# One block of a hybrid encoder: the mLSTM's matrix E scaled on VectorE alone, its transposes issued behind the next scores, the values' constant factor moved, the memory's steps in halves, and one step more in the gates' preparation

## The chip, the core and the metric

The kernel runs on one core of a Trainium2 chip, as one launch, in fp32. The metric is device time of one execution, in microseconds (us); the figure given for a kernel is the median over its runs. A profiled execution also gives a trace: every instruction of the engines TensorE (PE for matmuls, PEld for its weight loads), VectorE (DVE), ScalarE (ACT), GpSimd (POOL) and the DMA queues, with start, duration and what ended the idle time before it.

## The reference, cut to what matters

One layer over 512 tokens of width 1024, with three token mixers beside each other (a bidirectional mLSTM, a neighbourhood attention, a cross-attention into 256 memory tokens), a gated merge, and a convolutional feed-forward network. The change touches the mLSTM, 4 heads of width 128, forwards and backwards:

```python
q = q * (Dh ** -0.5)
inter_log = a + m_prev
m_j = max(inter_log, max(D))                    # D: causal log weights
P = exp(D - m_j) * (q @ k.T)
inter_w = exp(inter_log - m_j)
num = P @ v + inter_w * (C_prev @ q)
den = sum(P) + inter_w * (n_prev . q)
h = num / max(abs(den), exp(-m_j))
...
h = h_fw + h_bw
h = h * rsqrt(mean(h * h) + EPS) * norm_g
return sigmoid(o_pre) * h
```

The states C and n are carried from chunk to chunk: `C_new = decay * C + (wt * v)^T k`, `n_new = decay * n + wt^T k`.

## The kernel before

**The stream of matmuls.** Tokens lie along the free axis (512 columns), channels on the 128 partitions. Each projection is a sum over 8 slices of the width; each slice is three matmuls of 128x512 (`mm3`, L213 to L215), since weight and input are each held as a high and a low part. The low times low product is left out. The weights come in blocks by DMA; ACT makes the high part of a block (`wh`, L195), DVE the low part (`wl`, L196), one block ahead of the matmuls that use it. So TensorE has one long stream, and ACT and DVE supply it.

**The mLSTM between the projections.** The gates' preparation and the four heads are a generator, `ml_prep` and `ml_all`, that gives up control at every `yield`. The function `step(n)` adds n to a quota and runs one piece of the generator for each whole unit in it. The projections call it: `xaq` adds 1.25 behind each of its four tiles (`RB`), `o`, `naq` and `nak` add 1.25 a tile in quarters (behind slices 1, 3 and 5, and at the end), `memk` and `memv` add 0.7 a tile (`RM`), and the merge gates of the first branch add 1 a tile. What a piece issues stands behind the projection's matmuls issued so far, and ahead of those that follow; a scheduler then lays down an order for each engine, in which an instruction may come somewhat earlier or later than its place in the program. On each engine the order is then fixed. Some small work is put into a list, `late`, and issued by `flush()` at slices 1, 3 and 5 of a projection.

**The pieces.** The preparation has four: the log forget gates; the running sums and maxima, which are written to memory by two DMAs (`rd`); an empty one; then `pm`, which transposes the sums back (L616, read by ACT L620 and L621, where `em` holds the exponential of the negative maxima), together with the first head's `keys`. `keys` loads the two rows `R` of that head by DMA, spread over the partitions (queue of SP), transposes k (L676) and splits it. `spread`, run from `late`, spreads the chunk ends by a matmul (L629), copies them (L632) and makes the weights `wt`, the decays `dec` and the factors `num` from them (L634 to L650). Then each head has five pieces: `states`, and `weights_J` for the chunks J of 128 tokens, 0 to 3.

- `states` weighs the values (L694, L697, L698), makes the four chunk products (L716 and the `mm3` of 258 columns), and from them the running states C (ACT L728, DVE L730). For the first head it also adds the causal mask to `R` (L670).
- `weights_J` issues the scores (`kq`, L750) and the product with the state (L756, or an `mm3` of 258 columns). DVE multiplies W, which ACT made by exponentials (L740), by the scores and sums each row (L764), then takes the larger of the sum's absolute value and `em` (L767, L768), the reciprocal (L769) and the factors r (L770). ACT scales one direction of W into E (L771), DVE adds the other (L772). The part from the state goes to H (ACT L776, DVE L778).
- `turn_J` transposes E on TensorE (L786), and ACT copies the result back (L787). `values_J` multiplies it by the values `va` (L792), adds (L793) and sums squares (L795).
- Behind a head come the norm (DVE L799, the power on POOL L801, ACT L806) and `emit_y` (four transposes L814, L816, and the split for the output projection L219, L220).

A constant of the reference, 128^-0.5 / 4 in this kernel's scaling (`C_ML`), is a factor of the values `va`, of the row sums in L764, and, inverted, of the table `num`, which has a second half for E.

Of the kernel before, what the change touches and what calls it, by code (L numbers as in the profile page):

```python
# [17 lines left out]
P = 128  # L18
# [10 lines left out]
WARM = 14  # L29
RM, RB = 0.7, 1.25  # L30
RATE = 1.0
# [79 lines left out]
def hybrid_block(ctx, tc, xg, xT, memT, wflat, vecs, gbias, nabias, outa, outb, outc):  # L111
# [338 lines left out]
    SY.dma_start(gbf, gbias.partition_broadcast(P))  # L450
    rcc = cp.tile([P, NT], F32, name="rcc")
    V.tensor_scalar(rcc, rc, C_ML, None, op0=ALU.mult)

# [47 lines left out]
    va = va_u.rearrange("p (t h c) -> p t h c", t=4, h=4)  # L501
    G.memset(va[:, :, :, 128:129], C_ML)
    nav_d = dp.tile([S, 1024], F32R, name="nav_d")
    for c in range(3):
        n, nk = TMC[c], TMK[c]
        pss = [(mmps if c % 2 else atps)() for _ in range(NT)]
        for h in range(KT // nk):
            ws = weights(("tm", c, h))
            for t in range(NT):
                tsl = slice(t * P, (t + 1) * P)  # L510
                for k in range(nk):
                    kk = nk * h + k
                    ps = pss[t][:, :n]
                    mm3(ps, XH[kk][:, tsl], XL[kk][:, tsl], ws[k][0], ws[k][1], kk == 0, kk == KT - 1)
        for t in range(NT):
            ps = pss[t]
            if c == 0:
                V.scalar_tensor_tensor(Gt[:, t, :], ps[:, :16], rc[:, t:t + 1], gb, op0=ALU.mult, op1=ALU.add)
            if c < 2:
                o = 16 if c == 0 else 0  # L520
                A.activation(va[:, t, 2 * c:2 * c + 2, 0:128],
                             ps[:, o:o + 256].rearrange("p (h c) -> p h c", h=2), AF.Copy, scale=rcc[:, t:t + 1])
# [26 lines left out]
    def ml_prep():  # L549
# [48 lines left out]
        with tc.issue_after(st["pool"]):  # L598
            G.memset(cu[:36], 0.0)
        num = cp.tile([P, 2, 2, 4, 4], F32, name="num")  # L600
        with tc.issue_after(st["pool"]):
            G.memset(num, 1.0 / C_ML)
        V.tensor_tensor_scan(cu[0:4, :], on[0:4, :], lr[0:4, :], 0.0, op0=ALU.mult, op1=ALU.add)
# [7 lines left out]
        yield  # L611
        yield
        pm = atps()
        pmv = pm[:, :400].rearrange("p (t c) -> p t c", t=NT)
        for t in range(NT):
            PE.transpose(pmv[:, t, :], mr[:100, t * P:(t + 1) * P], ident[:100, :100])  # L616
        em = cp.tile([P, NT, 36], F32, name="em")
        cp.tile([P, NT, 30], F32, name="gap2")

        A.activation(lfc, pmv, AF.Copy)  # L620
        A.activation(em, pmv[:, :, 0:36], AF.Exp, scale=-1.0)  # L621

        def spread():
# [18 lines left out]
            br = cp.tile([P, 2, 4, 4], F32, name="br")  # L642
            sc = [num[:, 1, 0, 1:4], num[:, 1, 1, 0:3]]
            for d in range(2):
# [11 lines left out]
    def ml_all():  # L656
# [48 lines left out]
        def states(h, k, w, C, q, R, ee):  # L705
# [6 lines left out]
            at = lambda J, d: pc[J // 2][:, po[J] + 129 * d:po[J] + 129 * d + 129]  # L712
            for J in range(NT):
                if J in (0, 3):
                    e = J // 3
                    PE.matmul(at(J, e), ke[:, e * P:(e + 1) * P], ew[e], start=True, stop=True)  # L716
# [26 lines left out]
        def weights_J(H, ss, h, J, k, w, C, q, R, ee):  # L743
# [5 lines left out]
            kq = ps[:, 384:512]  # L749
            PE.matmul(kq, qT[:, hs], kT[:, hs], start=True, stop=True)  # L750
            if len(ds) == 2:
                qs = slice((J - 1) * P, J * P)
# [5 lines left out]
            E = ee[:, J % 2 * 256:J % 2 * 256 + 256].rearrange("p (x c) -> p x c", x=2)  # L758
            y = tiny(8)
            init, den, r = y[:, 0:2], y[:, 2:4], y[:, 4:8].rearrange("p (x d) -> p x d", x=2)  # L760
            dd = slice(ds[0], ds[-1] + 1)
            V.tensor_tensor(init[:, dd], pi[:, dd, 128], num[:, 1, dd, J, h], op=ALU.mult)
            for d in range(2):
                V.tensor_tensor_reduce(W[:, d, :], W[:, d, :], kq, C_ML, init[:, d:d + 1] if d in ds else 0.0,  # L764
                                       ALU.mult, ALU.add, accum_out=den[:, d:d + 1])
# [3 lines left out]
            V.reciprocal(den, den)  # L769
            V.tensor_tensor(r, num[:, :, :, J, h], den.unsqueeze(1).to_broadcast([P, 2, 2]), op=ALU.mult)  # L770
            A.activation(E[:, 0, :], W[:, 0, :], AF.Copy, scale=r[:, 0, 0:1])  # L771
            V.scalar_tensor_tensor(E[:, 0, :], W[:, 1, :], r[:, 0, 1:2], E[:, 0, :], op0=ALU.mult, op1=ALU.add)  # L772
            src = None
            for d in ds:
                if src is None:
                    A.activation(H[:, js], pi[:, d, 0:128], AF.Copy, scale=r[:, 1, d:d + 1])  # L776
                else:
                    V.scalar_tensor_tensor(H[:, js], pi[:, d, 0:128], r[:, 1, d:d + 1], src, op0=ALU.mult, op1=ALU.add)  # L778
                src = H[:, js]
# [51 lines left out]
        for h in range(4):  # L831
# [261 lines left out]

    def paced(key):
        return proj(key, XH, XL, at={k: lambda: step(RB / 4) for k in (1, 3, 5)})

# [23 lines left out]
    for f in range(4):  # L1120
        ps = proj(("memk", f), MH, ML, M)
        V.tensor_tensor(mk[:, f * M:(f + 1) * M], ps[:, :M], mrb, op=ALU.mult)
        step(RM)
    pss = [mmps() for _ in range(2)]
    for i in range(4):
        ws = weights(("memv", i))
        for t in range(2):
            tsl = slice(t * P, (t + 1) * P)
            for k in range(2):
                kk = 2 * i + k  # L1130
                mm3(pss[t], MH[kk][:, tsl], ML[kk][:, tsl], ws[k][0], ws[k][1], kk == 0, kk == KT - 1)
        step(RM)
    for t in range(2):
# [3 lines left out]
    for f in range(4):  # L1137
        ps = paced(("naq", f))
        V.tensor_tensor(nq[:, f * S:(f + 1) * S].rearrange("p (b r c) -> p b r c", r=ROWS, b=4), rv(ps), rv(rb),
                        op=ALU.mult)  # L1140
        step(RB / 4)
    for f in range(4):
        ps = paced(("nak", f))
        V.scalar_tensor_tensor(nk[:, f * S:(f + 1) * S], ps, 0.125, rb, op0=ALU.mult, op1=ALU.mult)
        step(RB / 4)

# [378 lines left out]
```

## Time and profile before

| | |
|---|---|
| runs | 878.5, 881.27, 878.76 us |
| median | 878.76 us |
| profiled execution, its own time | 880.92 us |
| its span in the trace | 879.1 us |
| mean granted TensorE clock in it | 0.997 of full speed |

The span is the time from the first to the last instruction in the trace; 1.8 us of the profiled execution lie outside it. A row of a timeline gives the start, the duration, the engine, the line, what is written from what, the shape, and in brackets the idle time before the instruction with what ended it. Matmuls overlap: the time from one start to the next is what one costs, not its duration. Among rows of waits, the numbers are the total, the count and the longest. A row of windows has the stretch and its length, then busy time and count of PE, PEld, DVE, ACT and POOL, the granted clock of TensorE, the share of the DMA engines and their GB/s. The mLSTM lies between 100 and 245 us of the span.

### The profile page before, as it was taken

How to read it: one execution, taken by the hardware profiler on the slowest of the kernel's cores; microseconds unless marked ns; L12 is line 12 of the kernel's file. 1: busy time of each engine (PE TensorE's matmuls, PEld its weight loads, DVE VectorE, ACT ScalarE, POOL GpSimd, SP SyncE). 2: the span in 40 equal slices, each digit the busy share in tenths (PEclk: the TensorE clock that was granted, in tenths of full speed). 3: DMA queues.
4: the chain of work that ended last, by engine and by line, in shares of the span. 5: the costliest groups of instructions: out<-in, count | busy, mean ns of one | idle time of the engine just before them, and what ended most of it. 6: DMA issues, size and time to landing. Idle time of an engine off the chain costs nothing.

```text
span 879.1 us, 12264 instructions
## 1 busy us (share of the span) xinstructions
PE 869.4 (99%) x4287; PEld 734.7 (84%) x4287; DVE 598.3 (68%) x1316; ACT 476.4 (54%) x1005; POOL 125.1 (14%) x202
## 2 busy tenths in 40 slices
PE   9999999999999999999999999999999999999997
PEld 7898878888888888888888888888888888888887
DVE  7794788886667758898667649667633466666534
ACT  7563467775446658888634455444422344444532
POOL 0101100000071551700000001211100011111010
PEclk9999999999999999999999999999999999999999
DMA  8324633532252444533323432332233323222412
GB/s 280 99 78 156 198 116 84 163 121 85 85 144 79 113 129 141 159 112 109 120 89 108 142 103 86 102 114 96 66 101 97 120 97 96 96 96 91 127 47 97
DMA packets 39423, 99.82 MB, mean 114 GB/s; under 512 B 5689, under 2 KB 13881, under 8 KB 39361
## 3 DMA queue, kind: packets, MB, share of 16 engines
q1 hardware_dynamic: 31568, 92.32, 32.6%
q0 software_dynamic: 7360, 6.32, 3.4%
q8 instruction: 34, 0.56, 0.3%
q10 hardware_dynamic: 432, 0.39, 0.1%
q14 instruction: 29, 0.23, 0.1%
HBM read 94.80 MB, written 4.21 MB: 113 GB/s over the span
## 4 chain that ended last, share of the span: by engine, by line
PE 92%; DVE 3%; ACT 2%; DMA 2%; issue 1%; POOL 0%; SPq 0%; POOLq 0%; DVEq 0%
PE mm L215 27%; PE mm L213 27%; PE mm L214 27%; PE at L214 2%; PE at L213 2%; PE at L215 2%; DMA R<-rd 1%; PE at L953 1%; PE at L934 1%; PE at L915 0%; DVE wl L196 0%; PE at L916 0%; DMA wr<-wflat 0%; ACT wh L195 0%; PE at L1041 0%
## 5 line engine op out<-in xcount | busy, mean ns | idle before, releaser
L213 PE MATMUL mm<-u,wh 128*128 128x512 f32 (+1 forms) x1072 | 415.4, 388 | 0.1
L215 PE MATMUL mm<-u,wl 128*128 128x512 f32 (+1 forms) x1072 | 412.2, 385 | 0.0
L214 PE MATMUL mm<-u,wh 128*128 128x512 f32 (+1 forms) x1072 | 412.2, 385 | 0.0
L195 ACT ACTIVATE wh<-wr 128x512 fp32r<-128x512 f32 (+2 forms) x298 | 184.7, 623 | 213.3 <-PE mm L214 169.1
L196 DVE TENSOR_TENSOR wl<-wr,wh 128x512 fp32r<-128x512 f32 (+3 forms) x300 | 204.3, 682 | 91.5 <-ACT wh L195 87.9
L215 PEld LDWEIGHTS mm<-u,wl 128*128 128x128 f32 x1072 | 201.6, 188 | 40.1 <-DVE wl L196 0.2
L214 PEld LDWEIGHTS mm<-u,wh 128*128 128x128 f32 x1072 | 202.0, 188 | 38.5
L213 PEld LDWEIGHTS mm<-u,wh 128*128 128x128 f32 x1072 | 201.7, 188 | 38.6 <-ACT wh L195 0.5
L1389 POOL TENSOR_TENSOR s<-s,rb 128x512 f32<-128x512 f32 x22 | 38.1, 1734 | 402.5 <-DVE s L1388 238.9
L542 POOL DMA_DIRECT2D u<-nav_d x128 | 62.3, 506 | 67.4 <-PE at L953 22.4
L219 ACT ACTIVATE u<-s 128x512 fp32r<-128x512 f32 x26 | 16.5, 634 | 59.8 <-DVE s L1392 56.2
L1392 DVE TENSOR_TENSOR s<-mm,s 128x512 f32<-128x512 f32 x22 | 15.2, 691 | 23.9 <-POOL s L1389 23.9
L462 ACT ACTIVATE s<-pad,vec 128x512 f32<-128x512 f32 x30 | 24.5, 816 | 9.8 <-DVE pad L460 9.8
L220 DVE SCALAR_TENSOR_TENSOR u<-s,u 128x512 fp32r<-128x512 f32 x26 | 19.1, 734 | 14.1 <-ACT u L219 14.0
L463 DVE SCALAR_TENSOR_TENSOR s<-pad,vec,s 128x512 f32<-128x512 f32 x30 | 22.5, 751 | 5.6 <-ACT s L462 5.5
L1388 DVE SCALAR_TENSOR_TENSOR s<-s,s 128x512 f32<-128x512 f32 x22 | 15.2, 691 | 13.4 <-ACT s L1387 13.3
L464 DVE SCALAR_TENSOR_TENSOR s<-pad,vec,s 128x512 f32<-128x512 f32 x30 | 22.5, 751 | 0.8
L1387 ACT ACTIVATE s<-s 128x512 f32<-128x512 f32 x22 | 14.0, 634 | 14.9 <-DVE s L1386 14.9
L460 DVE TENSOR_TENSOR pad<-mm,rb 128x512 f32<-128x512 f32 x22 | 15.1, 690 | 6.3 <-PE mm L215 6.2
L1167 DVE TENSOR_TENSOR s<-mm,rb_x 128x512 f32<-128x512 f32 x16 | 11.0, 689 | 12.1 <-PE mm L215 12.1
L1399 DVE TENSOR_TENSOR u<-mm,u 128x512 f32<-128x512 f32 x13 | 9.0, 692 | 14.6 <-PE mm L215 14.6
L213 PE MATMUL mm<-wh,u 128*128 128x512 f32 x48 | 18.8, 392 | 0.0
(338 smaller groups left out, 1077.6 us busy)
## 6 DMA issues: line engine op xcount, KB each, us to landing
wr<-wflat SPq DMA_DIRECT2D x141, 512.0 KB, 3.4
nab<-nabias SPq DMA_DIRECT2D x16, 256.0 KB, 2.9
u<-nav_d POOLq DMA_DIRECT2D x128, 32.0 KB, 2.8
s<-xT SPq DMA_DIRECT2D x15, 256.0 KB, 4.0
wr<-wflat SPq DMA_DIRECT2D x14, 192.0 KB, 2.4
nav_d<-nv POOLq DMA_DIRECT2D x8, 256.0 KB, 3.4
R<-rd SPq DMA_DIRECT2D x8, 256.0 KB, 5.0
wr<-wflat SPq DMA_DIRECT2D x2, 544.0 KB, 3.4
```

What stands on the lines that cost most here:

```text
L195: A.activation(h[:, u:v], src, AF.Copy)
L196: V.tensor_tensor(l[:, u:v], src, h[:, u:v].bitcast(F32), op=ALU.subtract)
L213: PE.matmul(ps, lh, rh, start=start, stop=False)
L214: PE.matmul(ps, lh, rl, start=False, stop=False)
L215: st["mm"] = PE.matmul(ps, ll, rh, start=False, stop=stop).ins
L219: A.activation(h, src, AF.Copy, scale=scale)
L220: V.scalar_tensor_tensor(l, src, scale, h.bitcast(F32), op0=ALU.mult, op1=ALU.subtract)
L462: A.activation(t1, pad[:, 0:512], AF.Identity, scale=vcol(w, i), bias=vcol(b, i))
L463: V.scalar_tensor_tensor(t1, pad[:, 1:513], vcol(w, n + i), t1, op0=ALU.mult, op1=ALU.add)
L464: V.scalar_tensor_tensor(t1, pad[:, 2:514], vcol(w, 2 * n + i), t1, op0=ALU.mult, op1=ALU.add)
L542: G.dma_start(vw[r * 32:(r + 1) * 32, i * 256:(i + 1) * 256], nav_v[hf, r, CW[b]:CW[b] + 32, hp * 256:(hp + 1) * 256])
L1389: G.tensor_tensor(c, c, rb2, op=ALU.mult)
```

## The change

1. The values lose their constant factor: `va` is scaled by the plain norm `rc`, its extra column is 1, and the operation on `rcc` goes. The row sums in L764 take a factor 1. In its place `em` is multiplied by 1/C_ML on DVE, once, in a new operation of 128x144.
2. `num` loses the half for E and its memset on POOL. E's first direction is scaled on DVE by the reciprocal itself (new L770), the second is added behind it (new L771), and r for the state's part is made by a `tensor_tensor` between the two (new L772). ACT's L771 goes.
3. `turn_J` moves into `weights_J`, behind the next chunk's scores; it was ahead of `emit_y` and of `weights_J`.
4. The products in `states` come in the order of chunks 0, 3, 1, 2.
5. The preparation has one empty piece more. `memk` and `memv` add their 0.7 in two halves, `naq` and `nak` add 1.3 a tile (`RN`).
6. An unused filler tile in the small pool grows from 30 to 40 columns.

```diff
-RM, RB = 0.7, 1.25
+RM, RB, RN = 0.7, 1.25, 1.3
...
-    rcc = cp.tile([P, NT], F32, name="rcc")
-    V.tensor_scalar(rcc, rc, C_ML, None, op0=ALU.mult)
...
-    G.memset(va[:, :, :, 128:129], C_ML)
+    G.memset(va[:, :, :, 128:129], 1.0)
...
-        num = cp.tile([P, 2, 2, 4, 4], F32, name="num")
-        with tc.issue_after(st["pool"]):
-            G.memset(num, 1.0 / C_ML)
...
         yield
         yield
+        yield
         pm = atps()
...
+        V.tensor_scalar(em, em, 1.0 / C_ML, None, op0=ALU.mult)
...
-            for J in range(NT):
+            for J in (0, 3, 1, 2):
...
             PE.matmul(kq, qT[:, hs], kT[:, hs], start=True, stop=True)
+            if open_J:
+                turn_J(*open_J[0])
...
-                V.tensor_tensor_reduce(W[:, d, :], W[:, d, :], kq, C_ML, init[:, d:d + 1] if d in ds else 0.0,
+                V.tensor_tensor_reduce(W[:, d, :], W[:, d, :], kq, 1.0, init[:, d:d + 1] if d in ds else 0.0,
...
-            V.tensor_tensor(r, num[:, :, :, J, h], den.unsqueeze(1).to_broadcast([P, 2, 2]), op=ALU.mult)
-            A.activation(E[:, 0, :], W[:, 0, :], AF.Copy, scale=r[:, 0, 0:1])
-            V.scalar_tensor_tensor(E[:, 0, :], W[:, 1, :], r[:, 0, 1:2], E[:, 0, :], op0=ALU.mult, op1=ALU.add)
+            V.tensor_scalar(E[:, 0, :], W[:, 0, :], den[:, 0:1], None, op0=ALU.mult)
+            V.scalar_tensor_tensor(E[:, 0, :], W[:, 1, :], den[:, 1:2], E[:, 0, :], op0=ALU.mult, op1=ALU.add)
+            V.tensor_tensor(r[:, dd], num[:, dd, J, h], den[:, dd], op=ALU.mult)
...
-                turn_J(*open_J[0])
                 if J == 2 and last:
                     emit_y(h - 1, last[0])
                 open_J.append(weights_J(*prev, h, J, *own))
...
-        ps = proj(("memk", f), MH, ML, M)
+        ps = proj(("memk", f), MH, ML, M, at={3: lambda: step(RM / 2)})
...
-        step(RM)
+        step(RM / 2)
...
-        step(RM)
+            step(RM / 2)
...
-    ps = paced(("naq", f))
+    ps = paced(("naq", f), RN)
```

The matmuls are as many as before (4107 rows of TensorE). DVE has 17 rows more, ACT 18 fewer. Three places in the order of the engines follow; in the names, the number behind a name tells one buffer from another.

The first is DVE around the preparation's end, where `wt` is made and the first head's values are weighed: `at` is what L629 (new L626) spread, `R` the rows with their mask, `u_1294` (new `u_1291`) the split k, `s` and `ee` the weighed values. Before:

```order
L639 TENSOR_TENSOR bi<-Gt,lfc 128x16 x2
L645 TENSOR_TENSOR br<-lfc 128x16 x2
L670 TENSOR_TENSOR R_1284<-R_1284,msk_132 128x512
L685 TENSOR_TENSOR u_1294<-mm_1289,u_1294 128x256
L632 COPY mt<-at_1301 128x64
L670 TENSOR_TENSOR R_1286<-R_1286,msk_127 128x512
```

A few small rows make `wt` and `dec`, and then:

```order
L196 TENSOR_TENSOR wl_1373<-wr_1183,wh_1372 128x512
L670 TENSOR_TENSOR R_1357<-R_1357,msk_132 128x512
L694 TENSOR_SCALAR s_1295<-u_597,wt 128x129
L698 SCALAR_TENSOR_TENSOR u_1294<-u_597,wt,u_1294 128x129 x2
L694 TENSOR_SCALAR ee_1288<-u_597,wt 128x129
```

Now, the same stretch:

```order
L618 TENSOR_SCALAR em<-em 128x144
L683 TENSOR_TENSOR u_1291<-mm_1286,u_1291 128x256
L636 TENSOR_TENSOR bi<-Gt,lfc 128x16 x2
L643 TENSOR_TENSOR br<-lfc 128x16 x2
L668 TENSOR_TENSOR R_1281<-R_1281,msk_132 128x512
L629 COPY mt<-at_1315 128x64
L668 TENSOR_TENSOR R_1283<-R_1283,msk_127 128x512
```

```order
L196 TENSOR_TENSOR wl_1413<-wr_1225,wh_1412 128x512
L692 TENSOR_SCALAR s_1292<-u_595,wt 128x129
L696 SCALAR_TENSOR_TENSOR u_1291<-u_595,wt,u_1291 128x129 x2
L692 TENSOR_SCALAR ee_1285<-u_595,wt 128x129
L696 SCALAR_TENSOR_TENSOR u_1291<-u_595,wt,u_1291 128x129 x2
L668 TENSOR_TENSOR R_1401<-R_1401,msk_132 128x512
```

The split of k stands ahead of the first mask, not between it and the copy; the mask of the second head stands behind the weighed values, not ahead. On TensorE, the chunk products that read them (L716, new L714) come behind 24 matmuls of the `o` projection, where they came behind 19.

The second is DVE at the first head's third chunk: from the reciprocal (L769) to E (L772, new L771) and H (L778). Before:

```order
L769 RECIPROCAL y_1543<-y_1543 128x2
L762 TENSOR_TENSOR y_1601<-at_1598,num 128x1
L670 TENSOR_TENSOR R_1685<-R_1685,msk_132 128x512
L770 TENSOR_TENSOR y_1543<-num,y_1543 128x4
L764 ISA E_1555,y_1601<-E_1555,at_1598,y_1601 128x128
L764 ISA y_1601 128x1
L764 ISA E_1555,y_1601<-E_1555,at_1598 128x128
L764 ISA y_1601 128x1
L1116 TENSOR_SCALAR u_1404<-s_1571 128x512
L772 SCALAR_TENSOR_TENSOR ee_1288<-E_1479,y_1543,ee_1288 128x128
L778 SCALAR_TENSOR_TENSOR H_1412<-at_1538,y_1543,H_1412 128x128
```

Now:

```order
L769 RECIPROCAL y_1574<-y_1574 128x2
L770 TENSOR_SCALAR ee_1285<-E_1526,y_1574 128x128
L772 TENSOR_TENSOR y_1574<-num,y_1574 128x2
L771 SCALAR_TENSOR_TENSOR ee_1285<-E_1526,y_1574,ee_1285 128x128
L1105 TENSOR_TENSOR s_1608<-mm_1556,rb_x 128x512
L778 SCALAR_TENSOR_TENSOR H_1439<-at_1567,y_1574,H_1439 128x128
```

E follows the reciprocal by three rows on one engine; the mask, the next chunk's sums and the output gate's last operation no longer stand between.

The third is TensorE at the end of the last head: L792 makes the last values, L814 are the transposes of `emit_y`, and the rows between are the merge gates' projection. Before, the values are followed by twelve matmuls on `wh_2631` and twelve on `wh_2672` (with `wl_2673`), of which the first and the last stand here:

```order
L792 MATMUL at_2604<-u_597,ee_2312 128x128
L213 MATMUL mm_2680<-u_149,wh_2631 128x512
...
L215 MATMUL mm_2680<-u_149,wl_2632 128x512
L213 MATMUL mm_2730<-u_147,wh_2672 128x512
...
L215 MATMUL mm_2730<-u_147,wl_2673 128x512
L814 MATMUL at_2743<-ident,H_2440 128x128 x4
```

Now by twelve in all:

```order
L792 MATMUL at_2624<-u_595,ee_2340 128x128
L213 MATMUL mm_2716<-u_149,wh_2668 128x512
...
L215 MATMUL mm_2716<-u_149,wl_2669 128x512
L814 MATMUL at_2755<-ident,H_2451 128x128 x4
L213 MATMUL mm_2783<-u_1945,wh_2708 128x512
```

The transposes stand twelve matmuls closer to the values that they need.

More of the change, by code (lines that the diff above doesn't have):

```diff
@@ L521, in hybrid_block @@
                 A.activation(va[:, t, 2 * c:2 * c + 2, 0:128],
-                             ps[:, o:o + 256].rearrange("p (h c) -> p h c", h=2), AF.Copy, scale=rcc[:, t:t + 1])
+                             ps[:, o:o + 256].rearrange("p (h c) -> p h c", h=2), AF.Copy, scale=rc[:, t:t + 1])
             if c > 0:
@@ L617, in ml_prep @@
         em = cp.tile([P, NT, 36], F32, name="em")
-        cp.tile([P, NT, 30], F32, name="gap2")
+        cp.tile([P, NT, 40], F32, name="gap2")
         A.activation(lfc, pmv, AF.Copy)
         A.activation(em, pmv[:, :, 0:36], AF.Exp, scale=-1.0)
+        V.tensor_scalar(em, em, 1.0 / C_ML, None, op0=ALU.mult)
         def spread():
@@ L642, in spread @@
             br = cp.tile([P, 2, 4, 4], F32, name="br")
-            sc = [num[:, 1, 0, 1:4], num[:, 1, 1, 0:3]]
+            num = cp.tile([P, 2, 4, 4], F32, name="num")
+            sc = [num[:, 0, 1:4], num[:, 1, 0:3]]
             for d in range(2):
@@ L758, in weights_J @@
             E = ee[:, J % 2 * 256:J % 2 * 256 + 256].rearrange("p (x c) -> p x c", x=2)
-            y = tiny(8)
-            init, den, r = y[:, 0:2], y[:, 2:4], y[:, 4:8].rearrange("p (x d) -> p x d", x=2)
+            y = tiny(6)
+            init, den, r = y[:, 0:2], y[:, 2:4], y[:, 4:6]
             dd = slice(ds[0], ds[-1] + 1)
-            V.tensor_tensor(init[:, dd], pi[:, dd, 128], num[:, 1, dd, J, h], op=ALU.mult)
+            V.tensor_tensor(init[:, dd], pi[:, dd, 128], num[:, dd, J, h], op=ALU.mult)
             for d in range(2):
-                V.tensor_tensor_reduce(W[:, d, :], W[:, d, :], kq, C_ML, init[:, d:d + 1] if d in ds else 0.0,
+                V.tensor_tensor_reduce(W[:, d, :], W[:, d, :], kq, 1.0, init[:, d:d + 1] if d in ds else 0.0,
                                        ALU.mult, ALU.add, accum_out=den[:, d:d + 1])
@@ L775, in weights_J @@
                 if src is None:
-                    A.activation(H[:, js], pi[:, d, 0:128], AF.Copy, scale=r[:, 1, d:d + 1])
+                    A.activation(H[:, js], pi[:, d, 0:128], AF.Copy, scale=r[:, d:d + 1])
                 else:
-                    V.scalar_tensor_tensor(H[:, js], pi[:, d, 0:128], r[:, 1, d:d + 1], src, op0=ALU.mult, op1=ALU.add)
+                    V.scalar_tensor_tensor(H[:, js], pi[:, d, 0:128], r[:, d:d + 1], src, op0=ALU.mult, op1=ALU.add)
                 src = H[:, js]
@@ L1092, in hybrid_block, with paced @@
     gens.append(ml_all())
-    def paced(key):
-        return proj(key, XH, XL, at={k: lambda: step(RB / 4) for k in (1, 3, 5)})
+    def paced(key, rate=RB):
+        return proj(key, XH, XL, at={k: lambda: step(rate / 4) for k in (1, 3, 5)})
     xq = unit()
@@ L1137, in hybrid_block @@
     for f in range(4):
-        ps = paced(("naq", f))
+        ps = paced(("naq", f), RN)
         V.tensor_tensor(nq[:, f * S:(f + 1) * S].rearrange("p (b r c) -> p b r c", r=ROWS, b=4), rv(ps), rv(rb),
                         op=ALU.mult)
-        step(RB / 4)
+        step(RN / 4)
     for f in range(4):
-        ps = paced(("nak", f))
+        ps = paced(("nak", f), RN)
         V.scalar_tensor_tensor(nk[:, f * S:(f + 1) * S], ps, 0.125, rb, op0=ALU.mult, op1=ALU.mult)
-        step(RB / 4)
+        step(RN / 4)
     mg = []
```

## The prediction

> **What bounds the kernel now.** I read the page first, then the waits of TensorE, then the windows of the mLSTM's stretch, and last the timelines around each gap.
>
> ```profile
> PE 869.4 (99%) x4287; PEld 734.7 (84%) x4287; DVE 598.3 (68%) x1316; ACT 476.4 (54%) x1005; POOL 125.1 (14%) x202
> PE at L716 <- DVE s L694: 1.9, 1, 1.9
> PE at L786 <- DVE H L778: 1.2, 2, 1.0
> PE at L786 <- ACT wh L195: 1.0, 1, 1.0
> ```
>
> TensorE is busy for 99% of the span and the matmuls are as many afterwards, so only the gaps in its stream are to be won. The three longest kinds are all in the mLSTM: one wait for the weighed values, three for a transpose of E. DVE and ACT matter only where a row of theirs ends such a wait. The largest gap:
>
> ```profile
> 120.95 0.39 PE L215 MATMUL mm<-u,wl 128*128 128x512 f32 x1
> 121.18 0.39 PE L213 MATMUL mm<-u,wh 128*128 128x512 f32 x1
> 123.50 0.71 PE L716 MATMUL at<-s 128*128 128x129 f32 x2 [1.93 <-DVE s L694]
> ...
> 124.44 0.63 PE L214 MATMUL mm<-u,wh 128*128 128x512 f32 x1
> 124.86 0.63 PE L215 MATMUL mm<-u,wl 128*128 128x512 f32 x1
> 120.00:130.00 10.00, 8.07 (x35) 6.69 (x35) 8.33 (x28) 6.64 (x22) 0.00 (x0) 0.83 0.27 89
> ```
>
> A full-speed 128x512 matmul costs 0.23 us from start to start (120.95 to 121.18). L716 was due at 121.41 and came at 123.50: 2.09 us lost. Behind it the same matmul costs 0.42. The window's clock of 0.83 says that 0.17 x 10 = 1.7 us of clock are missing, which is half speed for about 3.4 us. So this one gap took 3.8 us in the profiled execution. The others:
>
> ```profile
> 146.07 0.39 PE L215 MATMUL mm<-u,wl 128*128 128x512 f32 x1
> 147.43 0.33 PE L786 MATMUL at<-ident,ee 128*128 128x128 f32 x1 [0.97 <-DVE H L778]
> ...
> 160.62 0.28 PE L214 MATMUL mm<-u,wh 128*128 128x256 f32 x1
> 161.94 0.30 PE L786 MATMUL at<-ident,ee 128*128 128x128 f32 x1 [1.04 <-ACT wh L195]
> ...
> 192.33 0.38 PE L792 MATMUL at<-u,ee 128*128 128x128 f32 x2
> 192.97 0.33 PE L786 MATMUL at<-ident,ee 128*128 128x128 f32 x1 [0.26 <-DVE H L778]
> 140.00:150.00 10.00, 9.03 (x50) 7.46 (x49) 9.07 (x38) 7.13 (x23) 0.84 (x1) 1.00 0.46 107
> ```
>
> Taking off what the matmul ahead costs (0.23 for 512 columns, 0.12 for 256, 0.11 for each of two passes of 128), the losses are 1.13, 1.20 and 0.42 us. The clock stayed at 1.00 through 140 to 150: a gap of 1.1 did not lower it, the one of 2.1 did. Together 2.09 + 1.13 + 1.20 + 0.42 = 4.84 us, and 1.7 of clock.
>
> **The first gap: where the weighed values come from.**
>
> ```profile
> 119.60 0.69 DVE L670 TENSOR_TENSOR R<-R,msk 128x512 f32<-128x512 f32 x1 [1.63 <-DMA R<-rd]
> 120.21 0.42 DVE L685 TENSOR_TENSOR u<-mm,u 128x256 fp32r<-128x256 f32 x1
> 120.55 0.21 DVE L632 COPY mt<-at 128x64 f32<-128x64 f32 x1
> ...
> 122.47 0.69 DVE L670 TENSOR_TENSOR R<-R,msk 128x512 f32<-128x512 f32 x1
> 123.07 0.29 DVE L694 TENSOR_SCALAR s<-u,wt 128x129 f32<-128x129 f32 x1
> ...
> 123.79 0.29 DVE L694 TENSOR_SCALAR ee<-u,wt 128x129 f32<-128x129 f32 x1
> ```
>
> DVE takes its rows in order. It stood 1.63 us idle at the first mask, until the DMA of `R` had landed at 119.60, with the copy of `mt`, on which `wt` hangs, behind that mask. Both versions issue that load with `keys` at the end of `xaq`, so I let the mask start at 119.60 again. What the change takes off DVE's path to the weighed values is two rows: the split of k (120.21 to 120.55, 0.34 us) now comes ahead of the mask, in the idle time, and the second head's mask (122.47 to 123.07, 0.60) comes behind. The new `em` row falls into the same 1.63 us and costs nothing here; without that cover it would cost its own 0.2 to 0.4. So `s` starts at 123.07 - 0.94 = 122.13. TensorE started 0.43 behind that row before (123.50 against 123.07), so it could start at 122.56; with five matmuls more ahead of it, it is due at 121.41 + 5 x 0.23 = 122.55. The first chunk product waits no longer. The second stands right behind now (chunks 0, 3, 1, 2), and reads `ee`, made 0.72 after `s`: ready at about 123.28, due at 122.55 + 0.22 = 122.77. That leaves a wait of 0.5 us, half of the 1.1 that the clock survived, so I keep the clock at full speed.
>
> The wait moves on partly. The state C of chunk 0 ends at
>
> ```profile
> 130.32 0.34 DVE L730 SCALAR_TENSOR_TENSOR C<-C,dec,at 128x129 f32<-128x129 f32 x1
> 130.72 0.49 PE L756 MATMUL at<-C,u 128*128 128x129 f32 x2
> 126.15 0.63 PE L716 MATMUL at<-ee,s 128*128 128x129 f32 x2
> ```
>
> that is, 4.5 us behind the start of the last chunk product (126.15 to 130.66). In the new order L756 stands 18 matmuls and one score behind it, 18 x 0.23 + 0.2 = 4.3 us, and DVE has rows of the `o` projection in between, as before. I take 0.4 us for it: nothing below, 1.0 above, if the second head's mask (0.60) falls into that chain too.
>
> **The three transposes.** Each gap ends with a chain that the change shortens:
>
> ```profile
> 159.03 0.16 DVE L770 TENSOR_TENSOR y<-num,y 128x4 f32<-128x4 f32 x1
> 160.71 0.39 ACT L771 ACTIVATE ee<-E,y 128x128 f32<-128x128 f32 x1
> 161.45 0.35 DVE L772 SCALAR_TENSOR_TENSOR ee<-E,y,ee 128x128 f32<-128x128 f32 x1
> 158.99 1.29 ACT L806 ACTIVATE H<-H,y 128x128 f32<-128x128 f32 x4 [1.37 <-POOL y L801]
> ```
>
> At 160 us the factors were there at 159.2, but ACT was in the norm's four scalings (to 160.28) and a weight split; E's first direction came at 160.71, its second at 161.45. On DVE alone E follows L770's place by one `tensor_scalar`, a small row and 0.35: ready by about 159.9, ahead of the 160.74 at which TensorE wanted it. At 146 a mask and the next chunk's sums stood between on DVE; they stand behind now. At 192 the hand-over to ACT and back goes. I take all three as gone, 1.13 + 1.20 + 0.42 = 2.75 us, and 0.1 for a last transpose that the new order puts close to its E; against it stands 0.16 for a like wait at 135 us, below.
>
> ```profile
> 135.21 0.40 PE L214 MATMUL mm<-u,wh 128*128 128x512 f32 x1
> 135.60 0.30 PE L786 MATMUL at<-ident,ee 128*128 128x128 f32 x1
> ```
>
> **What DVE takes over.**
>
> ```profile
> L771 ACT ACTIVATE ee<-E,y 128x128 f32<-128x128 f32 x16 | 6.3, 395 | 4.4 <-DVE y L770 4.2
> L772 DVE SCALAR_TENSOR_TENSOR ee<-E,y,ee 128x128 f32<-128x128 f32 x16 | 5.6, 349 | 3.7 <-ACT ee L771 3.7
> L694 DVE TENSOR_SCALAR s<-u,wt 128x129 f32<-128x129 f32 x4 | 1.1, 285 | 0.0
> 170.00:180.00 10.00, 10.00 (x57) 8.47 (x56) 9.86 (x37) 9.78 (x28) 0.00 (x0) 1.00 0.62 174
> ```
>
> ACT loses 16 x 0.395 = 6.3 us. The new `tensor_scalar` of 128x128 is not in the trace; its nearest row is L694, the same operation with a column more: 0.285, so 16 x 0.285 = 4.6 us on DVE. The bounds are 0.2 (the time from L694's start to the next one's, 123.07 to 123.26) and 0.35 (a two-input row, L772): 3.2 to 5.6 us. It lies beside TensorE's stream, which hides it as long as DVE has room. It has least at 170 to 180, with 9.86 of 10 us busy; TensorE lost nothing there, since the weight splits are a block ahead. Two chunks in 10 us add 0.6 there. I count nothing for it, and a rival below counts it. The factor moved into `em` and the memset that goes cost and bring nothing: they are off every wait shown.
>
> **The end of the last head.**
>
> ```profile
> 236.45 0.38 PE L792 MATMUL at<-u,ee 128*128 128x128 f32 x2
> ...
> 242.17 0.60 PE L814 MATMUL at<-ident,H 128*128 128x128 f32 x4
> 238.05 1.01 POOL L801 TENSOR_TENSOR y<-y,nhalf 128x4 f32<-128x4 f32 x1 [0.64 <-DVE y L799]
> 239.09 1.29 ACT L806 ACTIVATE H<-H,y 128x128 f32<-128x128 f32 x4 [1.50 <-POOL y L801]
> ```
>
> The norm's chain takes 239.09 + 1.29 - 236.45 = 3.9 us from the values to the last scaled chunk. There were 24 matmuls in it, 5.6 us; there are 12, so that the transposes are due 0.14 + 12 x 0.23 = 2.9 us behind. They go chunk by chunk, 0.11 each as other passes of 128: the last would come 2.9 + 0.33 = 3.2 behind and is ready at 3.9. That is a new wait of 0.7 us (0.4 to 1.0, by whether one of ACT's weight splits of 0.6 falls in front).
>
> **The sum.** New losses: 0.5 + 0.4 + 0.1 + 0.7 = 1.7 us. The 1.8 us of that execution outside its span I let stand. Against its 880.92: gained 4.84 + 1.7 + 0.16 = 6.7, so 880.92 - 5.0 = 875.9. The median of the runs is 878.76, 2.16 lower. The run of 881.27 stands near the profiled one, the other two near 878.6; the nearest thing that differs by such an amount is the 1.7 us of clock. I take it that the two lower runs kept the full clock. Against the median the clock's term then goes: 878.76 - 5.0 + 1.7 = 875.5. The two sums agree within 0.4, and I forecast 875.5, with 874.3 to 877.0 as this case's own range from the bounds above.
>
> The Trainium skill's page "TensorE: Matmul & The Clock Gate", section "Part 1: The HAM clock gate", has the clock switch between full and half rate by a free-running activity window of about 3.4 us, so that the same program may or may not be throttled. The stretch at half speed shown above, about 3.4 us, agrees. By that rule the two lower runs need not have paid; if they all had, the sum would be that of the first rival.
>
> **Rivals.**
>
> *A, more.* The runs of the median paid for the clock too, and differ from the profiled execution by something else; or the small new waits at the states and the end do not come. With the first, 6.7 gained less 1.7 lost: 878.76 - 5.0 = 873.8; with the second, 5.0 gained without the clock's term and nothing lost: 873.8 as well. For it: the trace shows one execution only, and it did pay. Against it: the two groups of runs lie 2.5 apart.
>
> *B, the first gap stays.* The mask that waits for `R` sets the chain, and that load may land later than 119.60, since its DMA shares queues with others; by a microsecond later the wait for `s` is 1 us, C follows, and the clock falls with them in some runs. Then of the 5.0 only the transposes' gain less the end's wait is left, 2.75 + 0.16 - 0.8 = 2.1: 876.7 without the clock's loss, 878.4 with it. For it: DVE was idle at that DMA for 1.63 us. Against: nothing in the change moves the load.
>
> *C, slower: DVE becomes the bound from the moment its rows per chunk fill what the matmuls leave.* E's chain is now wholly on DVE, in order, behind weight splits of 0.69 and masks; in the heads 1 to 3 ACT used to take a part of it while DVE split weights. If ten of the twelve transposes there each come 0.6 late (one split ahead of them), 6.0 us are lost, with the end's 0.7, and 2.9 gained at the old transposes and 0.5 at the first gap: 878.76 + 6.0 + 0.7 - 3.4 = 882.1. It decides once DVE is over about 9.9 of 10 us in a window, as it was at 170 to 180. For it: that row. Against: the same row had no loss on TensorE, and DVE's windows ahead show 8.3 and 9.1.
>
> *D, nothing.* The gaps only trade places: 878.8.
>
> **Chances.** The forecast 0.50, A 0.14, B 0.18, C 0.14, D 0.04. A measurement of this kernel can tell about 0.3%, 2.6 us, from no change: faster means below 876.1. A lies there whole, the forecast for three quarters of its range, B hardly: 0.14 + 0.38 + 0.02 = 0.54. Slower means over 881.4, which C reaches in about two thirds of its cases (nine late transposes or more): 0.10. The rest, 0.36, is no change. The range goes from 873.2, below A, to 878.6, above B; C and part of D lie outside.
>
> **What would show it.** In the new profile the wait at the chunk products (new L714) is at most 0.6 us and the clock around 120 to 130 is 1.00; a clock below that means that B holds. No wait of 0.3 us or more stands at L786, and one of 0.4 to 1.0 at L814 near 242 us. The new L770 takes 0.2 to 0.35 us. DVE is busy for some 4 to 5 us more and ACT for some 6 less. The forecast is wrong if waits at L786 add up to over 1 us (C), if `R`'s mask starts later than 120.5 (B), or if a gap appears outside 100 to 245 us, where I expect none.

## The result, and the profile after

| | before | changed |
|---|---|---|
| median of 7 runs | 880.53 us | 876.32 us |
| lowest to highest | 878.5 to 881.27 | 875.56 to 876.8 |
| profiled execution | 880.92 | 876.34 |
| its span | 879.1 | 874.6 |

The ratio is 0.9957, with a 95% interval of 0.9944 to 0.9969: 0.43% faster, 2.7 to 4.9 us. The forecast was 875.5. The median of before has risen from the 878.76 of three runs to 880.53 of seven, because four of the seven lie near 881; the experiments say why. One later execution of the changed kernel took 2262.04 us at a granted clock of 1.000 and is left out of every median here.

TensorE's waits in the changed kernel (total, count, longest), with the windows that answer to those of before; the row that stands apart is the kernel before at 160 to 170:

```profile
PE at L714 <- DVE s L692: 0.4, 1, 0.4
PE at L714 <- DVE ee L692: 0.3, 1, 0.3
120.00:130.00 10.00, 9.18 (x46) 7.29 (x45) 9.54 (x31) 8.44 (x27) 0.00 (x0) 1.00 0.45 154
140.00:150.00 10.00, 10.00 (x69) 9.08 (x69) 9.20 (x42) 6.93 (x21) 0.00 (x0) 1.00 0.58 157
160.00:170.00 10.00, 10.00 (x54) 8.61 (x53) 8.77 (x30) 7.96 (x23) 0.00 (x0) 1.00 0.54 155
170.00:180.00 10.00, 9.98 (x56) 8.39 (x55) 9.47 (x35) 8.20 (x26) 0.00 (x0) 1.00 0.50 163
```

```profile
160.00:170.00 10.00, 8.96 (x61) 8.07 (x60) 7.59 (x25) 7.25 (x20) 0.00 (x0) 1.00 0.47 159
```

No wait at the transposes (L786) is long enough to be listed; 140 to 150 and 160 to 170 are without a gap, where TensorE was busy for 9.03 and 8.96 of 10 us before. The clock is 1.00 from 120 to 130, where it was 0.83. What is left of the first gap stands in TensorE's timeline, and where it comes from in DVE's:

```profile
122.43 0.39 PE L215 MATMUL mm<-u,wl 128*128 128x512 f32 x1
123.25 0.46 PE L714 MATMUL at<-s 128*128 128x129 f32 x2 [0.43 <-DVE s L692]
123.97 0.46 PE L714 MATMUL at<-ee,s 128*128 128x129 f32 x2 [0.26 <-DVE ee L692]
```

```profile
118.40 0.23 DVE L618 TENSOR_SCALAR em<-em 128x144 f32<-128x144 f32 x1
118.55 0.42 DVE L683 TENSOR_TENSOR u<-mm,u 128x256 fp32r<-128x256 f32 x1
...
120.29 0.69 DVE L668 TENSOR_TENSOR R<-R,msk 128x512 f32<-128x512 f32 x1 [0.98 <-DMA R<-rd]
120.90 0.22 DVE L629 COPY mt<-at 128x64 f32<-128x64 f32 x1
...
122.83 0.28 DVE L692 TENSOR_SCALAR s<-u,wt 128x129 f32<-128x129 f32 x1
...
123.55 0.28 DVE L692 TENSOR_SCALAR ee<-u,wt 128x129 f32<-128x129 f32 x1
```

L714 was due at 122.43 + 0.23 = 122.66 and came at 123.25, 0.6 late; the second started 0.72 behind it, 0.5 later than the first's two passes of 0.11 allow. That is 1.1 us in all. DVE waits for the DMA of `R` as before, but it landed at 120.29, not 119.60. The new `em` row and the split of k lie in front of that wait. The new waits behind:

```profile
129.10 0.38 PE L748 MATMUL at<-u,u 128*128 128x128 f32 x2
129.62 0.49 PE L756 MATMUL at<-C,u 128*128 128x129 f32 x2
...
239.41 0.39 PE L215 MATMUL mm<-u,wl 128*128 128x512 f32 x1
239.75 1.21 PE L814 MATMUL at<-ident,H 128*128 128x128 f32 x4
240.71 0.48 PE L213 MATMUL mm<-u,wh 128*128 128x512 f32 x1
```

L748's two passes of 0.11 end at 129.32, L756 comes at 129.62: 0.3 for the state C. The four transposes of `emit_y` take 0.96 us from their start to the next matmul and came 0.1 late; before they took 0.35 (242.17 to 242.52): 0.7 lost in all. The new operation, in the rows of groups:

```profile
L770 DVE TENSOR_SCALAR ee<-E,y 128x128 f32<-128x128 f32 x16 | 4.8, 302 | 0.3
L771 DVE SCALAR_TENSOR_TENSOR ee<-E,y,ee 128x128 f32<-128x128 f32 x16 | 5.6, 347 | 0.0
PE 868.0 (99%) x4287; PEld 733.6 (84%) x4287; DVE 601.6 (69%) x1332; ACT 471.0 (54%) x989; POOL 125.1 (14%) x201
```

It takes 0.302 us. DVE is busy for 3.3 us more, with 16 rows more on the page (1316 before), and ACT for 5.4 us less, with 16 fewer (1005 before).

### The profile page after: what moved, and what is told of

It is laid out like the page before. It is cut to its first block, busy times and chain, and to the rows that moved or that the text cites. A ratio compares the mean times of both kernels' runs of the same rounds, so it can differ in the third digit from the quotient of the medians.

```text
span 874.6 us, 12276 instructions
## 1 busy us (share of the span) xinstructions
PE 868.0 (99%) x4287; PEld 733.6 (84%) x4287; DVE 601.6 (69%) x1332; ACT 471.0 (54%) x989; POOL 125.1 (14%) x201
## 4 chain that ended last, share of the span: by engine, by line
PE 93%; DVE 3%; DMA 1%; ACT 1%; issue 1%; POOL 0%; SPq 0%; POOLq 0%; ACTq 0%
PE mm L213 27%; PE mm L215 27%; PE mm L214 27%; PE at L214 2%; PE at L213 2%; PE at L215 2%; PE at L952 1%; DVE wl L196 1%; PE at L933 1%; DMA R<-rd 1%; DMA wr<-wflat 0%; PE at L914 0%; PE at L915 0%; PE at L1040 0%; PE at L792 0%
```

## The experiments

For every run the same four sums are read from TensorE's timeline, as above: the time from one start to the next, less what that step takes without a wait (0.23 for 512 columns, 0.12 for 256, 0.11 for 128, and 0.35 for the four transposes of L814). All in us:

| run | chunk products | C | transposes L786 | end L814 | median |
|---|---|---|---|---|---|
| before | 2.1, and the clock | 0 | 3.3 | 0 | 880.53 |
| changed | 1.1 | 0.3 | 0.4 | 0.7 | 876.32 |
| e0 before again | 2.9, and the clock | 0 | 3.0 | 0 | 880.28 |
| e1 E on ACT again | 0.6 | 0.3 | 0.9 | 0.7 | 876.65 |
| e2 only E on DVE | 1.9 | 0 | 0.6 | 0 | 876.61 |
| e3 steps as before | 1.0 | 0.2 | 2.5 | 0 | 877.33 |
| e4 turn ahead | 0.9 | 0.3 | 0.5 | 0.7 | 876.19 |
| e5 order 0123 | 1.6 | 0.2 | 0.4 | 0.7 | 876.05 |
| e6 second load later | 0 | 0.5 | 0.4 | 0.7 | 875.7 |
| e7 load, and 1.375 | 0 | 0.5 | 1.9 | 0 | 876.07 |
| e8 changed again | 0.5 | 0.3 | 0.4 | 0.7 | 876.26 |
| e9 1.301 | 0.4 | 0.3 | 0.4 | 0 | 874.87 |
| e10 1.301 and load | 0.3 | 0.3 | 0.4 | 0 | 875.22 |
| e11 H on DVE, steps as before | 1.1 | 0 | 1.7 | 0 | 876.44 |

A row's sums are of one execution, its median is of 5 to 10. That execution can lie off the median: e3's took 878.43 us, 1.1 above it, and e5's 877.09, the longest of its five. e0 to e3 ran beside each other, e4 to e7, and e8 to e10; the kernel before had medians of 879.0, 878.79 and 879.3 there, and 878.95 beside e11. Across these groups half a microsecond decides nothing.

**e0, the clock.** The kernel before, unchanged.

> The kernel before, unchanged, to see the granted clock of each run beside its time. If the two groups of its runs (near 878.6 and near 880.9) differ by the half-speed stretch behind the first gap, runs near 878.6 show a mean clock of 0.999 to 1.000 and runs near 880.9 one of 0.997 to 0.998. If something else parts them, the clock does not go with the time.

The ten runs part cleanly. Five at a mean clock of 0.998 took 880.66 to 882.04 us, five at 0.999 or 1.000 took 878.49 to 879.9. Of the 30 runs of the same kernel made beside them, eight at 0.998 took 880.2 to 881.06 and 22 at the higher figures 878.33 to 879.59. So about 1.8 us lie between two groups that the clock tells apart, and the half-speed stretch is worth 1.7. Both traces of this kernel are of the group at the lower clock; that the faster runs lack the stretch is read from their clock and time alone. In e0's own profiled execution, of 882.04, the load of `R` landed later still:

```profile
PE at L716 <- DVE s L694: 2.8, 1, 2.8
115.00:135.00 20.00, 17.22 (x84) 14.33 (x83) 15.88 (x56) 11.48 (x35) 0.00 (x0) 0.91 0.40 132
121.08 0.69 DVE L670 TENSOR_TENSOR R<-R,msk 128x512 f32<-128x512 f32 x1 [2.48 <-DMA R<-rd]
```

One landing at 119.60 and one at 121.08 gave gaps of 2.1 and 2.9 in the same program: the landing time is not a constant of the kernel.

**e1, E's first direction on ACT again.** Against the changed kernel:

```diff
-            V.tensor_scalar(E[:, 0, :], W[:, 0, :], den[:, 0:1], None, op0=ALU.mult)
+            A.activation(E[:, 0, :], W[:, 0, :], AF.Copy, scale=den[:, 0:1])
```

> The changed kernel with E's first direction on ACT again, all else as changed. If the hand-over between ACT and DVE made the waits for the transposes, waits at L786 come back, 1.0 to 2.8 us in all, and the time is 877.3 to 879.1. If only the rows that stood between on DVE (mask, next chunk's sums) made them, the time stays within 0.5 us of the changed kernel, 876.3.

876.65 (ratio to before 0.997, 0.996 to 0.998). The two waits that come back are 0.4 and 0.5:

```profile
PE at L786 <- DVE ee L771: 0.3, 1, 0.3
PE at L786 <- DVE H L778: 0.2, 1, 0.2
```

The waits lie just below what the hand-over theory asked for, and the time is within the 0.5 us of the other theory. In the changed order ACT could keep E at a cost of about half a microsecond of waits.

**e2, E on DVE and nothing else.** Against the kernel before:

```diff
-            A.activation(E[:, 0, :], W[:, 0, :], AF.Copy, scale=r[:, 0, 0:1])
+            V.tensor_scalar(E[:, 0, :], W[:, 0, :], r[:, 0, 0:1], None, op0=ALU.mult)
```

> The kernel before with E's first direction on DVE and nothing else changed. By the prediction's terms the three transposes' 2.75 us go, the first gap of 2.09 us and its clock stay: 1.5 to 2.8 us below the kernel before, and runs still in two groups. If DVE is too full to take E, no gain or a loss, with waits at L786.

876.61 (0.9974, 0.9964 to 0.9983), 2.4 us below the kernel before beside it. The transposes' waits fall from about 3 us to 0.6, the first gap stays:

```profile
121.66 0.39 PE L213 MATMUL mm<-u,wh 128*128 128x512 f32 x1
123.78 0.46 PE L716 MATMUL at<-s 128*128 128x129 f32 x2 [1.73 <-DVE s L694]
...
124.41 0.39 PE L214 MATMUL mm<-u,wh 128*128 128x512 f32 x1
124.64 0.39 PE L215 MATMUL mm<-u,wl 128*128 128x512 f32 x1
```

Here a gap of 1.9 us was followed by matmuls at the full step of 0.23. Two of the ten runs, 878.26 and 878.55, show a clock of 0.998 and 0.997, the other eight, 875.88 to 876.86, 0.999. With e1 this shows that for the transposes E's engine and the new order overlap: in these two programs either alone removes most of their waits. Neither is safe by itself, as the next run shows.

**e3, the steps as before.** Against the changed kernel: no third empty piece, `RN` 1.25, and the memory's 0.7 whole again.

```diff
-RM, RB, RN = 0.7, 1.25, 1.3
+RM, RB, RN = 0.7, 1.25, 1.25
...
         yield
         yield
-        yield
         pm = atps()
```

> The changed kernel without the added empty piece, with the memory's steps whole and 1.25 for naq and nak. By the prediction the first gap depends on DVE's rows and on the five matmuls more: here the products come earlier on TensorE, and the mask's DMA lands when it did, so the first gap is 1.2 to 2.2 us again, perhaps with the clock (0.82 to 0.9 in 120 to 130); the wait at the end (0.8) goes: 876.0 to 878.5. If the placement does nothing, the first gap is 0.9 as in the changed kernel and the time 875.5.

877.33 (0.9982, 0.9972 to 0.9991), inside the expected span, but not by the expected terms. The products waited 1.0, about as in the changed kernel (1.1): the copy of `mt` came ahead of the mask here (118.71 against 120.35), which the expectation had not foreseen. The end's wait went. What came back are waits at the transposes (here L785), 2.5 us, with E on DVE. The second head's first chunk, TensorE, then DVE, then ACT:

```profile
157.35 0.39 PE L747 MATMUL at<-u,u 128*128 128x128 f32 x2
158.54 0.33 PE L785 MATMUL at<-ident,ee 128*128 128x128 f32 x1 [0.81 <-ACT H L775]
```

```profile
156.80 0.35 DVE L770 SCALAR_TENSOR_TENSOR ee<-E,y,ee 128x128 f32<-128x128 f32 x1
```

```profile
156.44 1.28 ACT L805 ACTIVATE H<-H,y 128x128 f32<-128x128 f32 x4 [1.37 <-POOL y L800]
157.63 0.61 ACT L195 ACTIVATE wh<-wr 128x512 fp32r<-128x512 f32 x1
158.15 0.34 ACT L775 ACTIVATE H<-at,y 128x128 f32<-128x128 f32 x1
```

E was complete at 157.15. The transpose began at 158.54, right behind H on ACT (to 158.49), which stood behind the norm's scalings and a weight split, just where E had stood before. H reads other columns of the tile of PSUM that the transpose writes, and both the wait and the timing name it.

**e4, the transposes ahead again.** Against the changed kernel, the two lines go back to where they were:

```diff
-            if open_J:
-                turn_J(*open_J[0])
...
+                turn_J(*open_J[0])
                 if J == 2 and last:
```

> The changed kernel with the transposes ahead of the next scores again. The theory that the new place of the transposes hardly matters, since E is there in time: within 0.4 us of the changed kernel's 876.3, no wait over 0.3 at the transposes. The rival, that their place gave a part of the gain: waits of 0.5 to 1.5 us at the transposes, 876.8 to 877.8.

876.19 (0.997, 0.9958 to 0.9981), transposes 0.5, none over 0.3, as its theory had it. The place of the transposes gives nothing that these runs can tell. In the order on TensorE they move by a few rows only, since the scheduler puts them late in both.

**e5, the chunks' order.**

```diff
-            for J in (0, 3, 1, 2):
+            for J in range(NT):
```

> The changed kernel with the chunk products in the order 0, 1, 2, 3. The second short product is then six 258-column matmuls later (0.7 us), which would hide the wait for ee (0.3 to 0.5); C's chain of chunk 0 begins later by as much. Theory: the first gap shrinks to about 0.6 and the wait at C grows by 0.3 to 0.7, so within 0.4 us of 876.3. Rival, that the order gave part of the gain: 0.5 us or more slower.

876.05 (0.9963, 0.995 to 0.9976): no difference in time. The first gap did not shrink as expected; the mask started at 120.45, 0.16 later than in the changed kernel, and a second wait for the load followed, so the sums of this one execution do not tell the order's share apart.

**e6, the second head's load later.**

```diff
                 t = tp.tile([P, S], F32, tag="R", name=nm("R"), bufs=4)
+                if h == 1:
+                    V.tensor_copy(t[:, 0:1], em[:, 0, 0:1])
                 SY.dma_start(t, rd[d, h].partition_broadcast(P))
```

> The changed kernel, where the load of the second head's rows waits until em is made (one column of each tile is first written from em), so that the first head's load has the DMA engines to itself. Theory, that the first gap is set by when this load lands: it lands 1 us or more earlier, the waits at the chunk products (0.6 and 0.3) and at C (0.3) go, 875.0 to 875.4. Rival, that it lands late for another reason: the gap stays at 0.6 to 0.9.

875.7 (0.9965, 0.9951 to 0.9979), above the 875.0 to 875.4 that were expected. The products' gap is gone:

```profile
119.22 0.22 DVE L629 COPY mt<-at 128x64 f32<-128x64 f32 x1
...
119.41 0.69 DVE L670 TENSOR_TENSOR R<-R,msk 128x512 f32<-128x512 f32 x1
...
121.20 0.29 DVE L694 TENSOR_SCALAR s<-u,wt 128x129 f32<-128x129 f32 x1
121.40 0.28 DVE L694 TENSOR_SCALAR ee<-u,wt 128x129 f32<-128x129 f32 x1
```

The mask no longer waits for the DMA (no bracket on its row), and `s` is made 1.6 us earlier. Two things changed at once, however: the load has less beside it, and the scheduler put the copy of `mt` ahead of the mask. The wait for C did not go, it grew from 0.3 to 0.5: that part of the expectation failed. What then held C's chain was not tried.

**e7, with a denser pace.** e6 and `RN` 1.375.

> As the run before, and 1.375 a tile for naq and nak, which brings the last head's end half a tile earlier, so that 24 matmuls stand again between the last values and the transposes behind the norm. Theory: the wait of 0.8 us at L814 (new number) goes too, 874.2 to 874.8. Rival: the denser pieces cost as much elsewhere on DVE, 875.0 or more.

876.07 (0.9968, 0.9955 to 0.9981): the rival. The end's wait went, and 1.0 us at 184 and 0.5 at 211 and 222 came at the transposes, the first again behind ACT's H.

**e8 to e10, a rounding of the pace.** 5 for `xaq`, 5 for `o`, 8 x 0.7 for the memory and 32 quarters of 0.325 make 26. Added one by one in binary they make 25.99999999999997, so the piece due at the end of `nak` waits half a tile, and the last head's end falls twelve matmuls late. e9 is the changed kernel with

```diff
-RM, RB, RN = 0.7, 1.25, 1.3
+RM, RB, RN = 0.7, 1.25, 1.301
```

and e10 has the later load of e6 as well; e8 is the changed kernel itself, beside them.

> The changed kernel, unchanged, beside the two that follow on one chip: 875.5 to 876.8, no run at a clock below 0.999, the wait at L814 again.

> The changed kernel with 1.301 for 1.3 a tile. The quota's sum behind nak is 26 by the numbers, but adding 0.325 thirty-two times in binary gives 25.99999999999997, so that the piece due there waits half a tile. With 1.301 three steps at the end come twelve matmuls earlier and nothing else moves. Theory: the wait of 0.8 us at L814 goes and no other comes: 0.6 to 0.9 below the changed kernel beside it. Rival: the end is hidden or moves to the output projection behind it: within 0.2.

> As the run before, with the second head's load later. If the two are independent: 1.1 to 1.6 us below the changed kernel beside it, 874.6 to 875.0, with only the wait at C (0.4 to 0.7) left. If not, no better than the better of the two alone.

Medians 876.26 (eight runs, 875.46 to 877.45), 874.87 and 875.22; against the kernel before 0.9967 (0.9957 to 0.9977), 0.9958 (0.9942 to 0.9975) and 0.9952 (0.994 to 0.9965). In e9 the transposes of `emit_y` run without a wait:

```profile
238.72 0.60 PE L814 MATMUL at<-ident,H 128*128 128x128 f32 x4
```

The traces show the 0.7 us of the end gone and no new wait; the two traced executions differ by 0.67. The medians differ by 1.4, more than the 0.6 to 0.9 that were expected; with the intervals overlapping, the 0.7 is what is shown. One of e9's five runs, 878.47, had a clock of 0.998, and so had its profiled run of 874.87, whose windows show 1.00 in this stretch: to three digits the mean is a hint, and the windows decide. Two of e7's five runs also show 0.998 and are no slower than the others (876.41 and 876.04), and a run of the kernel before shows 0.948 at 879.07. The two changes do not add up, and e10 lies above the 874.6 to 875.0 of its theory: its products kept 0.3, a wait behind the first of the larger products, and e10 and e9 cannot be told apart. In e8 the mask began at 119.26, and the products waited 0.5 where the first trace of the same program had 1.1.

**e11, H on DVE.** Against e3, for the chunks with one direction:

```diff
-                if src is None:
+                if len(ds) == 1:
+                    V.tensor_scalar(H[:, js], pi[:, d, 0:128], r[:, d:d + 1], None, op0=ALU.mult)
+                elif src is None:
```

> The run with the steps as before, and the state's part H of chunks 0 and 3 made on DVE, not ACT. There the transpose of the second head's first chunk began 1.4 us after E was made, when ACT had made H behind the norm's four scalings and a weight split; H reads the same tile of PSUM that the transpose writes. Theory, that the transpose waits for H: this wait (1.0 us near 158) goes, while the two behind H of chunks 1 and 2 (0.87 and 0.69, DVE L777 there) stay; 876.2 to 876.6. Rival, that something else in E's chain is late: the wait stays within 0.3 of 1.0 us.

876.44 (0.9968, 0.9956 to 0.9981): the time lies in the theory's span, but the waits fit neither side. The one near 158 stayed, at 1.3 us, as the rival had it; the wait near 143 went and that near 196 fell to 0.3. The scheduler had put a weight split between, on DVE:

```profile
155.79 0.15 DVE L771 TENSOR_TENSOR y<-num,y 128x1 f32<-128x1 f32 x1
157.16 0.69 DVE L196 TENSOR_TENSOR wl<-wr,wh 128x512 fp32r<-128x512 f32 x1 [1.22 <-ACT wh L195]
157.77 0.35 DVE L770 SCALAR_TENSOR_TENSOR ee<-E,y,ee 128x128 f32<-128x128 f32 x1
158.03 0.35 DVE L775 TENSOR_SCALAR H<-at,y 128x128 f32<-128x128 f32 x1
```

and on TensorE:

```profile
158.43 0.33 PE L787 MATMUL at<-ident,ee 128*128 128x128 f32 x1 [1.10 <-DVE H L775]
```

`wl` waits for ACT's `wh`, which stands behind the norm. The norm's scalings reach the transpose here by a third way, through E and H both. Most of this wait is E's own lateness, so the edit did not test what it was made for. But here too the transpose began right behind H, 0.05 after its end at 158.38, with E complete at 158.12.

**H in all the traces.** What this edit left open, the fourteen traces answer by their timing. Of 42 transposes of E in them that lost more than 0.14 us, 35 began 0.05 to 0.06 us behind the end of H, and seven began 0.14 to 0.15 behind the end of E. In the kernel before, two of the three long waits ended with H, not with E; the one at 146 us:

```profile
146.76 0.35 DVE L772 SCALAR_TENSOR_TENSOR ee<-E,y,ee 128x128 f32<-128x128 f32 x1
147.02 0.35 DVE L778 SCALAR_TENSOR_TENSOR H<-at,y,H 128x128 f32<-128x128 f32 x1
```

E was complete at 147.11, H at 147.37, and the transpose began at 147.43. At 192 it was 192.65, 192.91 and 192.97. At 160 it was E: complete at 161.80, with H done at 161.35, and the transpose at 161.94. The two waits of 0.2 in the changed kernel, at 135 and 172 us, end 0.06 behind H as well. No edit took H alone out of the way; the timing carries this.

## Why the prediction was right, point by point

The time, 876.32, lies in the range and in the likeliest case's own, 0.8 above the forecast of 875.5. By the steps:

- **The first gap.** Right in its mechanism: the load of `R` sets DVE's chain, the split of k and the second mask are off it. `s` was forecast at 122.13 with a landing at 119.60; it came at 122.83 with a landing at 120.29, both 0.7 later. "I let the mask start at 119.60 again" is the step that was mis-sized: the losses here were 1.1 for 0.5, and the sign given for this gap, at most 0.6 of waiting, was missed (0.4 and 0.3 are listed). That nothing in the change moves the load was not quite so either. The load was issued at 115.45, where it was at 115.26, and the next weight block's load followed at 118.51, where it came at 122.61. In e8 that block followed at 118.17 and the mask still began at 119.26, so the block alone does not explain it; why the load took longer stays open. e8, with a mask at 119.26, has the forecast's picture: hardly a wait for `s` (0.06), 0.5 for `ee` (forecast 0.5). Rival B described the landing as a risk; over the two traces of each kernel it lay between 119.26 and 121.08, but in the changed kernel it cost 0.6, not 1 and the clock.
- **The clock.** Right as far as is shown: the two groups of runs differ by 1.8 us and by a clock that fits the half-speed stretch (e0), and the changed kernel's seven runs show 0.999 or 1.000. The 4.2 us between the medians of 7 runs hold this term in part, since four of before's seven, by their times of 880.53 and more, had paid it. Against before's runs near 878.6 the gain is 2.3, where 3.3 was forecast.
- **C.** Forecast 0.4, measured 0.3.
- **The three transposes.** All three gone, as forecast; what stays is two waits of 0.2, where one of 0.1 was counted and 0.16 of before's was counted as gone. The reason was half of it. I put the gain down to E's place on DVE at two of the three, and to the order at one; e2 and e1 show that either suffices for most. What the prediction had no term for is H. Its own lines name H (L778) at 146 and 192, and there E was complete 0.3 us ahead of the transpose; only at 160 did E come last. At those two H stands right behind E on DVE, so an earlier E brings an earlier H. In e3, with E on DVE, a transpose waited 1.0 us for H on ACT, against 1.2 for E at 160 before. That the new steps would keep H out of the way was not foreseen, and is luck: undoing them took the waits at the transposes from 0.4 to 2.5 us.
- **DVE's new rows.** 0.302 each against 0.285; hidden, as forecast. DVE's busy time grew by 3.3 us where 4 to 5 were forecast, and ACT's fell by 5.4 where 6 were. Rival C did not come: DVE's 9.5 of 10 us in 170 to 180 left TensorE its work (9.98 of 10).
- **The end.** Forecast 0.7, measured 0.7. With this and the 1.1 at the products the new small waits came, so rival A fell in its second form.
- **The sum.** Forecast 875.9 for the profiled execution, measured 876.34; the 0.4 is mainly the products' 1.1 for 0.5, less small terms.

Outside 112 to 262 us the two programs lose the same, but for 0.3 us at the start, between 3 and 6 us, which the change does not touch.

## What to carry to other kernels

When a chain is taken off an engine, look at all that the consumer waits for: by the timing of the traces the transpose waits for the last reader of its PSUM tile as well as for its operand, and in half of the chunks that reader stayed in the old queue. Two edits that remove the same wait do not add up, so try each alone before crediting either. A pace that is summed in steps of 0.325 should not depend on reaching a whole number exactly.

## What the runs showed of the hardware that was not expected

The same load in the same program landed at 119.60 in one execution of the kernel before and at 121.08 in another, and the changed kernel's mask began at 120.29 and 119.26: a spread of about 1.5 and 1.0 us, as large as the gaps at issue. Why it varies was not tried.

Gaps of 2.1 and 2.9 us in the kernel before were followed by half speed, one of 1.9 in e2's profiled execution was not. Two of e2's ten runs showed a lower clock; they were not traced, so their gaps may have been longer. Whether a gap's length alone decides is therefore open. The free-running activity window which the Trainium skill's page "TensorE: Matmul & The Clock Gate", section "Part 1: The HAM clock gate", describes could part such runs too; no run here varied the phase of such a window.

A transpose that writes one part of a PSUM tile began 0.05 to 0.06 us behind the row that read another part of it, in 35 cases of the fourteen traces. In the changed kernel at 135 us its operand, E, had been complete for 1.8 us by then (134.10, H 135.82, the transpose 135.88).
